# Token places before pair weights, reads of the combined rows on SP and POOL, and weight buffers on the right

## The chip, the core and the metric

The kernel runs on one core of a Trainium2 chip. The metric is the device time of one execution in microseconds (us); less is better. The engines are PE (TensorE, matmuls), DVE (VectorE), ACT (ScalarE), POOL (GpSimd) and SP (SyncE, which here only issues DMAs and takes jumps). Each engine works off its own queue in order, and semaphores join the queues.

## The reference, cut to what matters

Two layers in sequence work on 512 tokens of 1024 values. The first ends in a hierarchical mixture of experts: a group of experts is chosen for each token, then two of its eight experts.

```
def hierarchical_moe(h, w_group, b_group, w_router, b_router, w_gate, w_up, w_down):
    t = h.reshape(-1, d)
    group_prob = softmax(t @ w_group + b_group)
    p_group, g_idx = lax.top_k(group_prob, 1)
    expert_logits = (t @ w_router + b_router).reshape(-1, N_GROUPS, EXPERTS_PER_GROUP)
    ...
    w_top, e_idx = lax.top_k(p_exp, TOP_K)                       # TOP_K = 2
    w_top = w_top / jnp.sum(w_top, axis=-1, keepdims=True) * p_group
    expert_ids = g_idx * EXPERTS_PER_GROUP + e_idx               # 32 experts
    for e in range(N_EXPERTS):
        hid = jax.nn.silu(t @ w_gate[e]) * (t @ w_up[e])         # 1024 -> 256
        out = out + combine[:, e:e + 1] * (hid @ w_down[e])      # 256 -> 1024

x = x + gate2[:, None, :] * ffn                                  # end of the first layer
f = swiglu(rms_norm_2(h, ffn1_norm_pre), ffn1_w_gate, ffn1_w_up, ffn1_w_down)
h = h + 0.5 * rms_norm_2(f, ffn1_norm_post)                      # start of the second
```

The second layer has two such FFNs (2816 wide) around an attention and recurrence mixer.

## The kernel before, in words

x lies in SBUF transposed, as eight tiles of 128 features by 512 tokens. `moe()` computes only the pairs of token and expert that were chosen. It first writes the normalised tokens as rows to DRAM (`h2d`, four DMAs on ACT's queue, line 1082). Routing on DVE gives `rank`, the place of each token in its expert's list (line 1135), and the weights of both experts (`w1`, `w2`, and `wa` spread over the experts).

The 32 experts are taken as eight quads of four. One pass serves the first 32 tokens of each of a quad's four experts, side by side in PE's columns: `expert1(q)` (line 1288) for gate and up, glu (lines 1278 to 1280), `turn` (1297), `expert2(q)` (1325) for down. An expert with more than 32 tokens has a conditional, `more(e)`, whose `wide_pass` serves the further ones; its condition is a count that each engine loads into a register (`count`, line 1380, jump on 1384). In this data a few of the conditionals are taken.

Which tokens stand in a quad is known in two ways. For quads 0 and 1 `select(q)` builds one-hot tiles of the ranks on DVE and multiplies them on PE with `val` (token number, weight, and token number plus 512 for the second choice; line 1227). For the others and for the wide passes a table in DRAM is used, `tab`: `fill_table` writes it with eight indirect scatters on POOL's queue (line 1208), and ACT's queue reads it back into `slots` (lines 1214 and 1202). Either way an indirect DMA on POOL's queue gathers the rows from `h2d` (line 1235) into `xg` for a quad or `htok0` to `htok3` for the wide passes; PE transposes them (1272), ACT and DVE scale them into `xgT` (1260, 1262).

Expert weights come as 192 loads of 512 KB on SP's queue into 30 rotating buffers, 13 in a pool at the left end of SBUF and 17 in one at the right end; a load waits until PE has used its buffer. Results are scattered into `yd` in DRAM, two rows for each token. The last quad's aren't: `combine` adds them by a matmul with one-hot tiles (`sq`, `ys`; lines 1308, 1309, 1313, 1373, 1374). What stands in `yd` is read by `fetch(i)` for 128 tokens at a time, two tiles each (line 1401); `collect(i)` adds both on POOL (1407), transposes on PE (1411) and adds into x on DVE (1415). The first three fetches use six spare weight buffers, the fourth the buffers of the first.

The order in each engine's queue is that of the program, but for what `issue_after` and a scheduler move within it. A conditional with jumps on all engines stands ahead of the last quad (line 1447).

The second layer's weights come as f32 tiles (`wraw`, line 251 on SP's queue), which ACT rounds to `wh` (line 257) and DVE to the rest `wl` (line 258); three matmuls for each product, on `xh`/`wh`, `xl`/`wh`, `xh`/`wl` (lines 274 to 276). `xh` and `xl` are made of x in lines 1590 and 1591. Their pool is `wp2`. The body's end, before:

```
self.xl = [self.t(self.ap, [P, S], f"xl{k}", F32R) for k in range(KT)]
self.wp = pool(s1, "wp2", 4, reuse_waits="tile")
self.even(self.wp, 480)
self.nsplit = 4
self.block2()
```

## Time and profile before

| | us |
|---|---|
| median of 3 runs | 2174.79 |
| lowest and highest run | 2173.87, 2176.84 |
| the profiled execution's own time | 2176.26 |
| its span in the profile | 2174.5 |
| PE busy in it | 1988.9 (91%) |
| DVE, ACT, POOL busy | 1041.9, 703.1, 220.5 |

The span is what the profiler saw of one execution; all starts in the rows count from its beginning. A share of busy time is a mean over stages with different limits, so what bounds a stage is read from that stage.

### The profile page before, as it was taken

What the parts mean: (1) busy time and instruction counts of PE and PEld (TensorE: products, weight loads), DVE (VectorE), ACT (ScalarE), POOL (GpSimd) and SP (SyncE); (2) the same over time, 40 slices, a digit from 0 to 9 for tenths busy, and PEclk for the clock granted to TensorE, in tenths of its full rate; (3) what the DMA queues carried; (4) which work ended last, traced back from release to release, by engine and by line L of the source; (5) the groups of instructions that cost most, each with busy time, mean ns of one, the idle gap of its engine ahead of it and who ended that gap; (6) DMA issues with size and microseconds to landing.
All of it is one profiled execution on the core that took longest, in us unless ns stands there. A gap on an engine that the chain in (4) does not pass through costs nothing. (4 is left out here: it accounts for less than half of the span.)

```text
span 2174.5 us, 32109 instructions
## 1 busy us (share of the span) xinstructions
PE 1988.9 (91%) x12778; PEld 1547.5 (71%) x12778; DVE 1041.9 (48%) x1901; ACT 703.1 (32%) x1173; POOL 220.5 (10%) x243
## 2 busy tenths in 40 slices
PE   5999999777777669999999999999999999999996
PEld 3677777544433348888888788888878888888885
DVE  4763664641111057552355674655664457542443
ACT  3532343122222114322233352524542244322231
POOL 3020002003212121000003200000000041000002
PEclk9999999888999879999999999999999999999998
DMA  7343215366999923333333132323233322333321
GB/s 268 117 127 115 84 58 182 131 229 227 405 394 390 359 83 107 97 89 100 103 97 98 56 100 77 118 63 107 69 102 92 112 69 88 97 93 101 97 87 40
DMA packets 110621, 294.94 MB, mean 136 GB/s; under 512 B 19995, under 2 KB 31387, under 8 KB 110444
## 3 DMA queue, kind: packets, MB, share of 16 engines
q1 hardware_dynamic: 98524, 271.78, 38.2%
q0 software_dynamic: 9856, 14.40, 2.1%
q10 hardware_dynamic: 2064, 6.37, 0.8%
q8 instruction: 113, 1.85, 0.3%
q14 instruction: 64, 0.52, 0.1%
HBM read 296.72 MB, written 17.90 MB: 145 GB/s over the span
## 5 line engine op out<-in xcount | busy, mean ns | idle before, releaser
L274 PE MATMUL mm<-xh,wh 128*128 128x512 f32 (+1 forms) x1584 | 614.6, 390 | 12.1 <-ACT wh L257 8.0
L275 PE MATMUL mm<-xl,wh 128*128 128x512 f32 (+1 forms) x1584 | 604.3, 382 | 4.8 <-DVE xl L1591 4.6
L276 PE MATMUL mm<-xh,wl 128*128 128x512 f32 (+1 forms) x1584 | 601.2, 381 | 0.5 <-DVE wl L258 0.5
L257 ACT ACTIVATE wh<-wraw 128x1024 fp32r<-128x1024 f32 (+3 forms) x282 | 274.0, 974 | 734.8 <-PE mm L275 645.2
L258 DVE TENSOR_TENSOR wl<-wraw,wh 128x1024 fp32r<-128x1024 f32 (+3 forms) x282 | 315.3, 1119 | 185.2 <-ACT wh L257 183.5
L274 PEld LDWEIGHTS mm<-xh,wh 128*128 128x128 f32 x1584 | 301.2, 191 | 78.1 <-ACT wh L257 9.3
L275 PEld LDWEIGHTS mm<-xl,wh 128*128 128x128 f32 x1584 | 302.1, 191 | 60.3 <-DVE xl L1591 6.4
L276 PEld LDWEIGHTS mm<-xh,wl 128*128 128x128 f32 x1584 | 301.2, 190 | 57.8 <-issue 2.0
L340 POOL TENSOR_TENSOR ss<-ss,sq 128x256 f32<-128x256 f32 (+1 forms) x69 | 66.5, 963 | 925.7 <-ACT sq L339 914.4
L274 PE MATMUL mm<-hh,wh 128*128 128x512 f32 (+1 forms) x416 | 148.5, 357 | 0.0
L276 PE MATMUL mm<-hh,wl 128*128 128x512 f32 (+1 forms) x416 | 148.3, 357 | 0.0
L275 PE MATMUL mm<-hl,wh 128*128 128x512 f32 (+1 forms) x416 | 148.2, 356 | 0.0
L1288 PE MATMUL mm<-wmoe,xgT 128*32 128x512 f32 x512 | 72.7, 678 | 26.2 <-DMA wmoe<-in_wmoe 20.3
L275 PEld LDWEIGHTS mm<-hl,wh 128*128 128x128 f32 x416 | 78.6, 189 | 11.4
L274 PEld LDWEIGHTS mm<-hh,wh 128*128 128x128 f32 x416 | 78.6, 189 | 11.3
L276 PEld LDWEIGHTS mm<-hh,wl 128*128 128x128 f32 x416 | 78.6, 189 | 11.2
L1279 DVE SCALAR_TENSOR_TENSOR mth<-mth,mm 128x256 f32<-128x256 f32 x8 | 3.4, 420 | 160.7 <-ACT mth L1278 160.7
L1651 DVE TENSOR_TENSOR sq<-mm,rsb 128x512 f32<-128x512 f32 x44 | 30.4, 691 | 103.9 <-PE mm L276 103.8
L1288 PEld LDWEIGHTS mm<-wmoe,xgT 128*32 128x32 f32 x512 | 20.2, 123 | 76.4 <-issue 40.2
L1646 DVE TENSOR_TENSOR cy<-mm,rsb 128x512 f32<-128x512 f32 x44 | 30.4, 691 | 85.4 <-PE mm L276 83.5
L1837 DVE TENSOR_TENSOR f<-mm,rsb 128x512 f32<-128x512 f32 x24 | 16.4, 688 | 52.1 <-PE mm L276 51.2
L1536 ACT ACTIVATE hh<-cy 128x512 fp32r<-128x512 f32 x44 | 27.9, 633 | 36.8 <-DVE cy L1652 36.8
(509 smaller groups left out, 2602.3 us busy)
## 6 DMA issues: line engine op xcount, KB each, us to landing
wmoe<-in_wmoe SPq DMA_DIRECT2D x192, 512.0 KB
wraw<-in_win SPq DMA_DIRECT2D x90, 512.0 KB
wraw<-in_wgu SPq DMA_DIRECT2D x88, 512.0 KB
wraw<-in_wada SPq DMA_DIRECT2D x32, 512.0 KB
wraw<-in_wd SPq DMA_DIRECT2D x32, 448.0 KB
big<-in_wada SPq DMA_DIRECT2D x16, 512.0 KB
wraw<-in_wd SPq DMA_DIRECT2D x16, 512.0 KB
wraw<-in_wout SPq DMA_DIRECT2D x16, 256.0 KB
```

The costliest lines, as they stand in the source:

```text
L257: self.nc.scalar.activation(h[:, :n], raw[:, :n], AF.Copy)
L258: self.nc.vector.tensor_sub(l[:, :n], raw[:, :n], h[:, :n])
L274: mm(ps, w1, xh[k], start=start and i == 0, stop=False)
L275: mm(ps, w1, xl[k], start=False, stop=False)
L276: mm(ps, w2, xh[k], start=False, stop=stop and i == nk - 1)
L340: self.nc.gpsimd.tensor_add(acc[:, hs], acc[:, hs], sq[:, hs])
L1279: v.scalar_tensor_tensor(th, th, 1.0, gate, op0=ALU.add, op1=ALU.mult)
L1288: self.end1 = mm(ps[cs].rearrange("p a b c -> p (a b c)"), xT[k // 4][:, k % 4, cs], piece(ws[c], k), start=k == 0, stop=k == KT - 1, tile ...
L1536: self.nc.scalar.activation(h, src, AF.Copy, scale=0.5)
L1646: v.tensor_mul(t1, pp[0], rb)
L1651: v.tensor_mul(t2, pp[1], rb)
L1837: v.tensor_mul(dst, ps, rb)
```

## The change: what it does

Routing. `val` loses its weight column, so it no longer needs the weights. `select(0)` stands right behind `rank`, then the gather of quad 0's rows; the weights (`pair_weights`), the table's rows and `fill_table` follow. The weights of quads 0 and 1 are picked by matmuls of their own, `select_weights`, behind `gather(1)`. The one-hot tile of quad 0 lies in a buffer of its own. `count(0)` is issued behind the last scaling of `xgT` on DVE.

Fetch and collect. `fetch` goes from ACT's queue to SP's, the fourth to POOL's. The collects stand between the last quad's conditionals: 0 and 1 behind the second, 2 behind the third, 3 behind the fourth.

Buffers. `wp2` is made at the right end of SBUF, where the 17 weight buffers of the experts lay, and its tiles are laid out before use.

```diff
@@ -1140,51 +1140,56 @@
...
-        val = sm([P, 4, NE, 3], "val")
+        val = sm([P, 4, NE, 2], "val")
...
-        v.tensor_copy(val[:, :, :, 1], wa)
-        v.scalar_tensor_tensor(val[:, :, :, 2], a2, float(S), tokb.unsqueeze(2).to_broadcast([P, 4, NE]), op0=ALU.mult, op1=ALU.add)
...
+        v.scalar_tensor_tensor(val[:, :, :, 1], a2, float(S), tokb.unsqueeze(2).to_broadcast([P, 4, NE]), op0=ALU.mult, op1=ALU.add)
+
+        def pair_weights():
...
+        def table_rows(w1, w2):
...
+            return td, rows
...
-        def fill_table():
+        def fill_table(td, rows):
@@ -1216,20 +1221,31 @@
         def select(q):
 
-            oh = self.t(mp, [P, 4, 4, first], "oh")
+            oh = self.t(mp, [P, 4, 4, first], "oh") if q else q1.rearrange("p (a b c) -> p a b c", a=4, b=4)
             for i in range(4):
                 v.tensor_tensor(oh[:, i], iota[:, :first].unsqueeze(1).to_broadcast([P, 4, first]),
                                 rank[:, i, q::8].unsqueeze(2).to_broadcast([P, 4, first]), ALU.is_equal)
-            pv = self.pst([P, 3], "mm")
+            pv = self.pst([P, 2], "mm")
+            pick(oh, q, pv, val)
+            idu = self.t(mp, [P, 1], "idu", U32, bufs=2)
+            v.tensor_scalar_add(idu, pv[:, 0:1], BIG - 1.0)
+            idx = self.t(mp, [P, 1], "idy", U32, bufs=2)
+            v.tensor_scalar_add(idx, pv[:, 1:2], BIG - 1.0)
+            return idu, idx, oh
+
+        def pick(oh, q, out, vals):
             for i in range(4):
                 for c in range(4):
                     cs = slice(32 * c, 32 * c + 32)
-                    mm(pv[cs, :], oh[:, i, c, :], val[:, i, ex(q, c), :], start=i == 0, stop=i == 3, tile_position=(0, 32 * c))
-            idx = self.t(mp, [P, 1], "idy", U32, bufs=2)
-            v.tensor_scalar_add(idx, pv[:, 2:3], BIG - 1.0)
+                    mm(out[cs, :], oh[:, i, c, :], vals[:, i, ex(q, c)], start=i == 0, stop=i == 3, tile_position=(0, 32 * c))
+
+        def select_weights(q, oh):
+
+            pv = self.pst([P, 1], "mm")
+            pick(oh, q, pv, wa.unsqueeze(3))
             wv = self.t(mp, [P, 1], "wv", bufs=2)
-            v.tensor_copy(wv, pv[:, 1:2])
-            return idx, wv, pv
+            v.tensor_copy(wv, pv)
+            return wv
@@ -1238,9 +1254,7 @@
         def gather(q):
 
             if q < 2:
-                idx, wv, pv = select(q)
-                idu = self.t(mp, [P, 1], "idu", U32, bufs=2)
-                v.tensor_scalar_add(idu, pv[:, 0:1], BIG - 1.0)
+                idu, idx, wv = select(q)
@@ -1259,7 +1273,7 @@
-                    v.tensor_scalar(xTs[hf][:, k, :], pt[:, k, :], self.gs2[:, kk:kk + 1], mod[:, 3, kk:kk + 1], op0=ALU.mult, op1=ALU.add)
+                    self.fed = v.tensor_scalar(xTs[hf][:, k, :], pt[:, k, :], self.gs2[:, kk:kk + 1], mod[:, 3, kk:kk + 1], op0=ALU.mult, op1=ALU.add)
@@ -1398,7 +1412,7 @@
         def fetch(i, ys):
 
             for a in range(2):
-                nc.scalar.dma_start(ys[a], yd[a * S + i * P:a * S + (i + 1) * P, :])
+                (g_ if i == 3 else nc.sync).dma_start(ys[a], yd[a * S + i * P:a * S + (i + 1) * P, :])
             return ys
@@ -1415,10 +1429,14 @@
         gat = {0: gather(0)}
+        w1, w2, wa = pair_weights()
+        fill_table(*table_rows(w1, w2))
         xt = xpose(gat[0][0])
         gat[1] = gather(1)
-        fill_table()
-        count(0)
+        for i in range(2):
+            gat[i] = (*gat[i][:2], select_weights(i, gat[i][2]))
+        with tc.issue_after(self.fed.ins):
+            count(0)
         for c in range(4):
             gather_wide(ex(0, c))
         th = expert1(0, xt)
@@ -1461,10 +1479,10 @@
         for c in range(4):
             more(ex(q, c), late)
-        for i in range(4):
-            collect(i, got[i])
-            if i == 0:
-                got.append(fetch(3, got[0]))
+            for i in ((), (0, 1), (2,), (3,))[c]:
+                collect(i, got[i])
+                if i == 0:
+                    got.append(fetch(3, got[0]))
         expert2(q, hT, *gat[q][1:3], late)
@@ -1958,7 +1976,11 @@
-                self.wp = pool(s1, "wp2", 4, reuse_waits="tile")
+
+                self.even(pool(s1, "gap", reuse_waits="tile"), 480)
+                self.wp = pool(s1, "wp2", 4, side="right", reuse_waits="tile")
+                for n in ("wraw", "wh", "wl"):
+                    self.t(self.wp, [P, 1024], n, F32 if n == "wraw" else F32R, bufs=4)
                 self.even(self.wp, 480)
```

How it moves the instructions. On POOL's queue, at the first quad's gather: `tab` is the table, `xg` the rows of a quad, `htok` those of a wide pass, `h2d` the rows in DRAM. Before:

```order
L1208 DMA tab<-r_td_4881,r_rows_4892 17408x4 x7
L1235 DMA xg_4718<-h2d,idu_4941 128x1024
L1208 DMA tab<-r_td_4881,r_rows_4892 17408x4
L1235 DMA xg_4718<-h2d,idu_4992 128x1024
L1235 DMA htok_751_4735<-h2d,slots_804_4908 128x1024
```

And in the changed kernel:

```order
L1251 DMA xg_4718<-h2d,idu_4891 128x1024
L1213 DMA tab<-r_td_4920,r_rows_4931 17408x4 x8
L1251 DMA xg_4718<-h2d,idu_5013 128x1024
L1251 DMA htok_751_4735<-h2d,slots_793_4863 128x1024
```

The gather for quad 0 stood behind seven of eight scatters, and stands ahead of all of them now.

On ACT's queue, from the conditional ahead of the last quad to its wide pass: `wmoe` are spare weight buffers, `mth` is what glu makes. Before:

```order
L1401 DMA wmoe_8187<-yd 128x1024
L1401 DMA wmoe_8188<-yd 128x1024
L1401 DMA wmoe_8189<-yd 128x1024
L1401 DMA wmoe_8190<-yd 128x1024
L1401 DMA wmoe_8191<-yd 128x1024
L1401 DMA wmoe_8192<-yd 128x1024
L1401 DMA wmoe_8188<-yd 128x1024
L1278 ACTIVATE mth_14994<-mm_14961 128x256
L1299 COPY hT_15001<-mm_14998 128x256
```

And in the changed kernel:

```order
L1465 UNCONDITIONAL_BRANCH
L1292 ACTIVATE mth_15026<-mm_14993 128x256
L1313 COPY hT_15033<-mm_15030 128x256
```

The seven reads ahead of glu left ACT. On SP's queue of the changed kernel they stand behind the same jump, and the next layer's first loads (`wraw`) stand among the jumps of the last quad's conditionals, four more behind them:

```order
L1415 DMA wmoe_8219<-yd 128x1024
L1415 DMA wmoe_8220<-yd 128x1024
L1415 DMA wmoe_8221<-yd 128x1024
L1415 DMA wmoe_8222<-yd 128x1024
L1415 DMA wmoe_8223<-yd 128x1024
L1415 DMA wmoe_8224<-yd 128x1024
L1394 TENSOR_LOAD r_cmi_785_4848
...
L251 DMA wraw_15613<-in_wgu 128x1024
L251 DMA wraw_15619<-in_wgu 128x1024
L1398 COMPARE_AND_BRANCH
L1398 UNCONDITIONAL_BRANCH x2
L251 DMA wraw_15625<-in_wgu 128x1024
```

Before, SP had no read of `yd`, and all loads of `wraw` stood behind the four jumps and a load of `c_cols`. On ACT's queue, at the evictions of the last `expert2` (into `ys`), before:

```order
L1401 DMA wmoe_8187<-yd 128x1024
L1308 ACTIVATE ys_2059_15003<-mm_15453,slots_803_4907 128x512
L1308 ACTIVATE ys_2059_15003<-mm_15464,slots_803_4907 128x512
L339 ACTIVATE sq_15627<-x_68 128x256
```

And in the changed kernel:

```order
L257 ACTIVATE wh_15615<-wraw_15613 128x1024
L1322 ACTIVATE ys_2060_15035<-mm_15485,slots_792_4862 128x512
L257 ACTIVATE wh_15621<-wraw_15619 128x1024
L257 ACTIVATE wh_15627<-wraw_15625 128x1024
L1322 ACTIVATE ys_2060_15035<-mm_15496,slots_792_4862 128x512
L257 ACTIVATE wh_15633<-wraw_15631 128x1024
L339 ACTIVATE sq_15666<-x_68 128x256
```

Four splits of the next layer's weights (`wh`) now stand ahead of, between and behind the two evictions; before, they stood behind x's squares, among the making of `xh`.

## Rows read from the trace of the kernel before

**Rows 1.** Windows: stretch, its length, busy us of each engine, clock, DMA share, GB/s.

```profile
480.00:492.00 12.00, 0.61 (x32) 0.55 (x32) 4.00 (x28) 0.20 (x1) 6.77 (x7) 0.50 0.97 361
...
512.00:536.00 24.00, 21.37 (x123) 13.94 (x127) 2.70 (x8) 5.59 (x13) 4.60 (x5) 0.93 0.85 298
...
560.00:740.00 180.00, 138.22 (x800) 68.25 (x792) 24.72 (x70) 41.16 (x92) 35.40 (x36) 0.93 1.01 391
```

**Rows 2.** Timeline from routing to the first wide pass: start, length, engine, line, operation.

```profile
472.52 0.34 ACTq L1082 DMA_DIRECT2D h2d<-htok  x1
...
479.25 0.29 DVE L1135 SCALAR_TENSOR_TENSOR r_rank<-sm,r_aa 128x128 f32<-128x128 f32 x1 [1.42 <-PE sm L1132]
...
483.40 1.08 POOL L1208 DMA_INDIRECT tab<-r_td,r_rows  x1 [60.71 <-DVE r_td L1186]
...
484.39 0.61 PE L1227 MATMUL mm<-r_val,oh 128*32 128x3 f32 x32 [5.18 <-DVE r_val L1166]
...
491.21 0.97 POOL L1208 DMA_INDIRECT tab<-r_td,r_rows  x1 [0.30 <-issue]
492.05 0.16 DVE L1229 TENSOR_SCALAR idy<-mm 128x1 uint32<-128x1 f32 x1 [7.80 <-remote]
...
493.14 1.06 POOL L1235 DMA_INDIRECT xg<-h2d,idu  x1 [0.95 <-issue]
...
497.38 1.94 PE L1272 MATMUL mm<-c_ident,xg 128*128 128x128 f32 x8 [12.38 <-DMA xg<-h2d,idu]
...
499.69 8.81 PE L1288 MATMUL mm<-wmoe,xgT 128*32 128x512 f32 x64
...
500.00 0.15 DVE L1229 TENSOR_SCALAR idy<-mm 128x1 uint32<-128x1 f32 x1
...
502.82 1.01 POOL L1235 DMA_INDIRECT htok<-h2d,slots  x1 [0.73 <-issue]
...
512.89 1.38 PE L1272 MATMUL mm<-c_ident,htok 128*128 128x128 f32 x8 [1.80 <-ACTq L1384]
```

**Rows 3.** Timeline of the last quad, from its expert1 to the last collect.

```profile
745.27 8.91 PE L1288 MATMUL mm<-wmoe,xgT 128*32 128x512 f32 x64 [5.89 <-ACTq L1447]
...
754.48 10.75 ACTq L1401 DMA_DIRECT2D wmoe<-yd  x7
...
765.27 0.38 ACT L1278 ACTIVATE mth<-mm 128x256 f32<-128x256 f32 x1 [25.02 <-DMA wmoe<-yd]
...
768.53 1.94 PE L1272 MATMUL mm<-c_ident,htok 128*128 128x128 f32 x8 [1.17 <-ACTq L1384]
...
790.87 5.35 PE L1411 MATMUL mm<-c_ident,wmoe 128*128 128x128 f32 x24 [3.39 <-DVEq L1384]
...
796.74 2.34 POOL L1407 TENSOR_TENSOR wmoe<-wmoe,wmoe 128x1024 f32<-128x1024 f32 x1 [26.99 <-DMA wmoe<-yd]
...
799.14 1.10 PE L1411 MATMUL mm<-c_ident,wmoe 128*128 128x128 f32 x8 [2.92 <-POOL wmoe L1407]
```

**Rows 4.** Timeline from the last expert2 to the next layer's first matmul.

```profile
805.61 42.78 SPq L251 DMA_DIRECT2D wraw<-in_wgu  x12
805.62 0.69 ACT L1308 ACTIVATE ys<-mm,slots 128x512 fp32r<-128x512 f32 x1 [0.95 <-PE mm L1325]
...
807.01 6.35 DVE L1374 SCALAR_TENSOR_TENSOR x<-mm,mod,x 128x256 f32<-128x256 f32 x16
...
815.24 1.69 ACT L1590 ACTIVATE xh<-x,c_cols 128x256 fp32r<-128x256 f32 x4
...
816.83 1.04 ACT L257 ACTIVATE wh<-wraw 128x1024 fp32r<-128x1024 f32 x1
...
817.93 0.58 PE L274 MATMUL mm<-xh,wh 128*128 128x256 f32 x1 [5.96 <-ACT wh L257]
```

**Rows 5.** The page's costliest groups: two lines of the next layer's matmuls.

```profile
L274 PE MATMUL mm<-xh,wh 128*128 128x512 f32 (+1 forms) x1584 | 614.6, 390 | 12.1 <-ACT wh L257 8.0
...
L276 PE MATMUL mm<-xh,wl 128*128 128x512 f32 (+1 forms) x1584 | 601.2, 381 | 0.5 <-DVE wl L258 0.5
```

More of the change, by code (lines that the diff above doesn't have):

```diff
@@ L1141, in moe @@
         v.tensor_copy(cmi, cnt)
-        eg = sm([P, 4, 4], "eg")
-        v.tensor_sub(eg, Lg, gm.to_broadcast([P, 4, 4]))
-        s.activation(eg, eg, AF.Exp)
-        pg = sm([P, 4, 1], "pg")
-        v.tensor_reduce(pg, eg, axis=AX.X, op=ALU.add)
-        v.reciprocal(pg, pg)
-        w1, w2 = sm([P, 4, 1], "w1"), sm([P, 4, 1], "w2")
-        v.tensor_sub(w2, m2, m1)
-        s.activation(w2, w2, AF.Exp)
-        v.tensor_scalar_add(w1, w2, 1.0)
-        v.reciprocal(w1, w1)
-        v.scalar_tensor_tensor(w1, w1, 0.5, pg, op0=ALU.mult, op1=ALU.mult)
@@ L1170, in moe @@
-        td = sm([P, 4, 2, 4], "td")
-        tu = td.bitcast(U32)
-        slot = sm([P, 4, NE], "slot")
-        v.scalar_tensor_tensor(slot, rank, float(NE), iota[:, :NE].unsqueeze(1).to_broadcast([P, 4, NE]), op0=ALU.mult, op1=ALU.add)
-        s12, s2 = sm([P, 4, 1], "s12"), sm([P, 4, 1], "s2")
-        a12 = sm([P, 4, NE], "a12")
-        v.tensor_mul(a12, slot, a2)
-        v.tensor_reduce(s2, a12, axis=AX.X, op=ALU.add)
-        v.tensor_mul(a12, slot, aa)
-        v.tensor_reduce(s12, a12, axis=AX.X, op=ALU.add)
@@ L1180, in moe @@
-        v.tensor_sub(s12, s12, s2)
-        rows = self.t(mp, [P, 4, 2], "r_rows", U32)
-        for a, sa in enumerate((s12, s2)):
-            v.tensor_scalar_add(rows[:, :, a:a + 1], sa, -1.0 - NE)
-            v.tensor_scalar_add(tu[:, :, a, 0], tokb, BIG - 1.0)
-            v.tensor_scalar_add(tu[:, :, a, 1], tokb, BIG - 1.0 + a * S)
-            v.tensor_copy(td[:, :, a, 2:3], (w1, w2)[a])
-            v.tensor_scalar_add(td[:, :, a, 3], tokb, BIG)
+        val = sm([P, 4, NE, 2], "val")
@@ new lines, in moe @@
+        v.tensor_copy(val[:, :, :, 0], tokb.unsqueeze(2).to_broadcast([P, 4, NE]))
+        v.scalar_tensor_tensor(val[:, :, :, 1], a2, float(S), tokb.unsqueeze(2).to_broadcast([P, 4, NE]), op0=ALU.mult, op1=ALU.add)
+        def pair_weights():
+            eg = sm([P, 4, 4], "eg")
+            v.tensor_sub(eg, Lg, gm.to_broadcast([P, 4, 4]))
+            s.activation(eg, eg, AF.Exp)
+            pg = sm([P, 4, 1], "pg")
+            v.tensor_reduce(pg, eg, axis=AX.X, op=ALU.add)
+            v.reciprocal(pg, pg)
+            w1, w2 = sm([P, 4, 1], "w1"), sm([P, 4, 1], "w2")
+            v.tensor_sub(w2, m2, m1)
+            s.activation(w2, w2, AF.Exp)
+            v.tensor_scalar_add(w1, w2, 1.0)
+            v.reciprocal(w1, w1)
+            v.scalar_tensor_tensor(w1, w1, 0.5, pg, op0=ALU.mult, op1=ALU.mult)
+            v.tensor_mul(w2, w1, w2)
+            v.tensor_mul(o1, o1, w1.to_broadcast([P, 4, 8]))
+            v.tensor_mul(o2, o2, w2.to_broadcast([P, 4, 8]))
+            v.tensor_add(o1, o1, o2)
+            wa = sm([P, 4, NE], "wa")
+            outer(wa, o1)
+            return w1, w2, wa
@@ new lines, in table_rows @@
+        def table_rows(w1, w2):
+            td = sm([P, 4, 2, 4], "td")
+            tu = td.bitcast(U32)
+            slot = sm([P, 4, NE], "slot")
+            v.scalar_tensor_tensor(slot, rank, float(NE), iota[:, :NE].unsqueeze(1).to_broadcast([P, 4, NE]), op0=ALU.mult, op1=ALU.add)
+            s12, s2 = sm([P, 4, 1], "s12"), sm([P, 4, 1], "s2")
+            a12 = sm([P, 4, NE], "a12")
+            v.tensor_mul(a12, slot, a2)
+            v.tensor_reduce(s2, a12, axis=AX.X, op=ALU.add)
+            v.tensor_mul(a12, slot, aa)
+            v.tensor_reduce(s12, a12, axis=AX.X, op=ALU.add)
+            v.tensor_sub(s12, s12, s2)
+            rows = self.t(mp, [P, 4, 2], "r_rows", U32)
+            for a, sa in enumerate((s12, s2)):
+                v.tensor_scalar_add(rows[:, :, a:a + 1], sa, -1.0 - NE)
+                v.tensor_scalar_add(tu[:, :, a, 0], tokb, BIG - 1.0)
+                v.tensor_scalar_add(tu[:, :, a, 1], tokb, BIG - 1.0 + a * S)
+                v.tensor_copy(td[:, :, a, 2:3], (w1, w2)[a])
+                v.tensor_scalar_add(td[:, :, a, 3], tokb, BIG)
+            return td, rows
```

6 lines of the change are left out of this document (removed).

## The prediction

> **What bounds the kernel now.** I read the windows first. The mixture of experts is the stretch from about 480 to 800 us. From 560 to 740 the DMA share is 1.01 at 391 GB/s, so the weight loads bind there. From 512 to 536 it is 0.85, and the loads follow PE (TensorE), which frees their buffers [rows 1]. The change touches none of these bytes, so that stretch keeps its length and moves with its start. What can be won lies where neither loads nor PE are full: the start, before the first expert matmul, and the tail, after the last weights.
>
> Next the timeline of the start. The rank of each token in its expert is there at 479.25 + 0.29 = 479.54. Then all wait for the token rows of the first quad: PE selects at 484.39, POOL issues seven table scatters from 483.40 to 491.21, VectorE (DVE) reads the selection at 492.05, POOL gathers xg at 493.14, PE transposes xg at 497.38 and begins expert1(0) at 499.69 [rows 2]. POOL's order is what holds: with the places ready at 486, the gather would still stand behind the scatters.
>
> Then the timeline of the tail. PE ends the last quad's expert1 at 745.27 + 8.91 = 754.18. ScalarE (ACT) turns it into glu only at 765.27, after 25.02 us of idleness: ahead of glu on its queue stand seven reads of yd, 10.75 us from the first to the end of the seventh, which waits until POOL has added the first pair. The first wide pass follows at 768.53. Later the collects stop once more: the last pair is added at 796.74, its transposes follow at 799.14 [rows 3].
>
> Last, the handover to the next layer: x ends at 807.01 + 6.35 = 813.36, and PE starts FFN1 at 817.93, released by the weight split wh that ACT ran at 816.83 [rows 4].
>
> **The change part by part.** The sum is made against the profiled execution, 2176.26 us, 1.47 above the median of 2174.79, and moved to the median at the end.
>
> **Routing, the start.** Behind the rank now come four one-hot writes, each of the rank's size (0.29 by its row, 1.2 in all), the selection (0.61) and the reading of the place (0.16) [rows 2]. With 0.3 for three handovers idu is there at 481.8. The gather then waits for h2d, not for its places. The four writes of h2d, 2 MB, begin at 472.52 [rows 2] beside weight loads, in a stretch that moves 361 GB/s [rows 1]; with half of that for h2d they land 11.6 us later, at 484.1, my estimate. So POOL gathers at about 484.3 instead of 493.14.
>
> Its landing is bounded from both sides. From issue to transposes it took 497.38 - 493.14 = 4.2 with the DMA engines almost free, which gives 488.5. On the other side, the loads that fill the engines (share 0.97) belong to the stretch that ends at 492, and 512 KB more add 1.4 at 361 GB/s: 493.4 at the latest. I take 491.5, nearer to the full end. PE's transposes then come 5.9 earlier. Two further selections of one column, 0.61 each at the most, now stand on PE, and the last ACT feed stands behind the slot reads on ACT's queue; I take 0.4 off: **5.5 us**, with 2 and 8 as ends.
>
> Is that carried on? The scatters' pitch is (491.21 - 483.40) / 6 = 1.30. The eighth stood behind xg's gather, at about 494.4; now all eight stand behind it, 484.3 + 8 x 1.30 = 494.7. The wide gathers need the table back and so come 0.3 later, at 503.1 instead of 502.82. Rows gathered then are there 4.2 later, at 507.3. PE wants them 4.4 after the end of expert1(0) (512.89 less 499.69 + 8.81 [rows 2]); with that end near 502.9, at 507.3. It just carries. The count loads on SP come after the last feed now, which delays SP's next weight load only if they are not through when PE frees a buffer, near 505. The arithmetic of the pairs' weights moves behind the places, and nothing needs it before the evictions of expert2(0); cover: all of expert1(0). Without it, 4 us.
>
> **Fetch and collect, the tail.** With yd's reads on SP nothing stands ahead of glu: 754.3 instead of 765.27, **11.0 us**. The wide pass moves to 757.5, the collects from 790.87 to about 779.9. The reads wait for the same scatters and buffers on SP as on ACT, so I leave them at 754.48; the first three additions were done within 10 us of the seventh read and still end before the collects. The four conditionals cost what they did (their jumps show as most of the 3.39 before the collects), but a collect's part now waits for a jump on POOL, PE and DVE each. fetch(3) goes to POOL's queue, its second read behind two jumps. Before, its addition stopped PE for 2.92 [rows 3]; two jumps more lie in its chain now, and two jumps and two collects over it. I take 1 off for all that: **10 us**, with 5 and 11.5 as ends.
>
> A rule of the Trainium skill speaks against POOL as issuer. SBUF — State Buffer, section "SBUF: two separate sides", says that while certain VectorE operations hold the port that they share, GpSimd can't write the descriptors of its DMAs, and gives about 3.1 us instead of 0.62 for one; by it the two reads cost up to 5 more. The trace shows the scatter of 483.40, with DVE at work beside it, at 1.08, and the one of 491.21, with DVE idle, at 0.97 [rows 2]. That is 0.1 apart, and I price it at nothing.
>
> **Weight buffers at the other end, the handover.** The next layer's first weight tiles now lie over buffers that the last quad leaves sooner: in the order SP issues two loads ahead of the fourth conditional and four behind it, so by my estimate near 788 and not after the last expert, as at 805.61 [rows 4]. ACT's first four splits, and two of DVE's, stand around the last expert's evictions. The gain: PE waits for xh, of which the first would be ready near 815.24 + 0.42 = 815.7, and not for wh: 817.93 - 815.7 = 2.2. The cost: two splits of 1.04 stand ahead of the second eviction, which had 0.95 of idleness before it: 1.1, and x ends as much later [rows 4]. Net **1 us**; -3 if wraw lands late behind the reads of yd, 3 if the second eviction hides the splits.
>
> Sum: 5.5 + 10 + 1 = 16.5. That is 2159.8 for the profiled execution, and **2158 us** for the median (2174.79 - 16.5 = 2158.3).
>
> **The rivals.** (1) The start isn't carried. For it: PE's selection ended at 485.0 and DVE read it at 492.05, after 7.80 of idleness for which no engine of the core is named [rows 2]. If that delay belongs to the selection, idu comes near 489, the gather is 4 earlier, not 8.8, and the table, behind it now, is 5 later; 0 to 2 are left, and 2174.79 - 12 = 2163. Against: the second selection was read at 500.00 without such a wait. Chance 0.2. (2) The tail gives part back: the second eviction waits for wraw, or fetch(3) is late by the page's 5, or the jumps between the collects add up to 5. Each costs 4 to 6: 2163. For it speaks that each is a wait on a queue in order, with no other work behind it. Chance 0.15. (3) Both, or a change that doesn't do what it says, because the gather waits for the last loads and the splits for the last expert: 6 or less is left, 2169 to 2177. Chance 0.1. (4) Slower: the new place of the weight tiles makes the next layer's matmuls longer. L274, L275 and L276 have 1584 of the larger kind each, 4752, at 390 and 381 ns [rows 5]. Against a gain of 16.5 it decides from 16500 / 4752 = 3.5 ns each, 0.9%; at 1.5% it is 27 us and 2185. Against: L274 reads wh and L276 wl, tiles at different places, with 2% between them at the most, and L274 is the one that stands first behind each wait. Chance 0.1.
>
> That leaves 0.45 for the forecast.
>
> **How the numbers follow.** By its ends the forecast gains 11 to 22 (not all low ends at once): 2153 to 2164. The range takes in rivals (1) and (2) with their scatter and part of (3): 2151 to 2171 leaves out (4), half of (3) and a small chance of more. Within 0.2% is 4.35 us, about what can be told here from no change. Slower is (4), 0.1; the same is most of (3), 0.07; faster is the rest, 0.83.
>
> **What would show it.** In the changed kernel xg's gather stands ahead of every scatter on POOL, near 484, and expert1(0) begins near 494; if DVE reads the places near 492 all the same, it is rival 1. The first wide pass begins near 507. glu follows the end of the last expert1 within 0.5, and the last collect waits less than 3 for POOL. FFN1's first matmul follows x's end within 3.5, and from it to the end stay 2174.5 - 817.93 = 1356.6 us; if that grew, rival 4. Wrong is the forecast if the way from the rank to the first wide pass shrinks by less than 3, or if glu still waits.

## The result, and the profile after

The changed kernel takes **2160.74 us**, the median of 4 runs (2158.49 to 2163.64). The kernel before took 2175.72 beside it (4 runs), so the ratio is 0.9933, with an interval of 0.9916 to 0.995: faster by 15.0 us. The profiled execution has a span of 2160.6, against 2174.5 before. The forecast was 2158.0.

The start, in the timeline of the changed kernel (columns as in [rows 2]; the weight loads of SP and the last write of `h2d` are shown too):

```profile
478.67 0.29 DVE L1135 SCALAR_TENSOR_TENSOR r_rank<-sm,r_aa 128x128 f32<-128x128 f32 x1 [1.42 <-PE sm L1132]
...
479.41 0.33 ACTq L1082 DMA_DIRECT2D h2d<-htok  x1
...
480.60 0.14 DVE L1231 TENSOR_SCALAR idu<-mm 128x1 uint32<-128x1 f32 x1
...
480.89 33.21 SPq L1045 DMA_DIRECT2D wmoe<-in_wmoe  x10
...
484.73 1.13 POOL L1251 DMA_INDIRECT xg<-h2d,idu  x1 [62.58 <-DMA wmoe<-in_wmoe]
486.16 1.06 POOL L1213 DMA_INDIRECT tab<-r_td,r_rows  x1 [0.30 <-issue]
...
492.86 1.94 PE L1286 MATMUL mm<-c_ident,xg 128*128 128x128 f32 x8 [12.46 <-DMA xg<-h2d,idu]
...
496.83 0.16 PE L1240 MATMUL mm<-r_wa,cy 128*32 128x1 f32 x1 [0.56 <-issue]
...
497.80 0.16 DVE L1231 TENSOR_SCALAR idu<-mm 128x1 uint32<-128x1 f32 x1 [2.23 <-remote]
...
498.40 9.32 PE L1302 MATMUL mm<-wmoe,xgT 128*32 128x512 f32 x62
```

The places (`idu`) are there 1.9 after the rank. The gather of `xg` stands ahead of every scatter and is issued at 484.73, 5.3 after the last write of `h2d`. The row names a weight load as what it waited for. In E9 below, where the six last loads come later, the gather is issued 5.3 after that write too, so these loads are not what held it. Up to here the forecast holds (idu 481.8, gather 484.3). Then the rows land late: transposes at 492.86, 8.1 after the issue. From there to expert1(0) it takes another 5.5, of which more below. From the rank to the first wide pass nothing is won in this execution: 33.67, against 33.64 before.

The tail, in the same timeline (answers to [rows 3]):

```profile
745.01 8.69 PE L1302 MATMUL mm<-wmoe,xgT 128*32 128x512 f32 x64 [6.19 <-ACTq L1465]
...
753.78 0.38 ACT L1292 ACTIVATE mth<-mm 128x256 f32<-128x256 f32 x1 [14.08 <-PE mm L1302]
...
754.24 2.80 SPq L1415 DMA_DIRECT2D wmoe<-yd  x6
...
757.04 1.06 PE L1286 MATMUL mm<-c_ident,htok 128*128 128x128 f32 x8 [1.41 <-DVE sq L1327]
...
763.66 0.60 POOL L1415 DMA_DIRECT2D wmoe<-yd  x1 [0.30 <-POOL wmoe L1421]
...
777.59 0.57 POOL L1415 DMA_DIRECT2D wmoe<-yd  x1 [8.64 <-PE mm L1425]
...
780.85 1.06 PE L1425 MATMUL mm<-c_ident,wmoe 128*128 128x128 f32 x8 [2.69 <-DVEq L1398]
...
784.33 1.97 PE L1425 MATMUL mm<-c_ident,wmoe 128*128 128x128 f32 x8 [2.41 <-POOL wmoe L1421]
```

glu (753.78) follows the end of expert1 (745.01 + 8.69 = 753.70) by 0.08; before it came 11.1 after it. The wide pass begins at 757.04, forecast 757.5. The last collect stops for POOL for 2.41, forecast below 3. Between them is a gain that the forecast did not have. The windows of both kernels over the wide pass (columns: stretch, its length, busy us of PE, PE's weight loads, DVE, ACT and POOL, clock, DMA share, GB/s), before:

```profile
757.00:773.00 16.00, 5.13 (x16) 4.00 (x17) 4.62 (x7) 2.50 (x6) 6.99 (x3) 0.57 0.55 216
```

and after:

```profile
757.00:773.00 16.00, 15.48 (x64) 10.87 (x64) 6.04 (x13) 4.25 (x10) 7.62 (x4) 1.00 0.55 208
```

From the end of expert1 to the wide pass it was 14.4 us before (754.18 to 768.53), in which PE did two transposes only, and the granted clock of the stretch above was 0.57, a mean between the level of 1.2 GHz (0.50) and the full one. It is 3.3 now, with the same two transposes, and the clock stays at 1.00, which is 2.4 GHz. The same ten matmuls at the head of the wide pass, before:

```profile
770.41 3.65 PE L1340 MATMUL mm<-wmoe,cy 128*128 128x256 f32 x10
```

and after:

```profile
758.17 2.43 PE L1354 MATMUL mm<-wmoe,cy 128*128 128x256 f32 x10
```

The clock does not stay up in each kernel with this tail. E4, a run told below, has the same 3.3 us ahead of its wide pass, and yet the mean over the same stretch is 0.89:

```profile
752.00:768.00 16.00, 15.51 (x57) 10.93 (x58) 4.37 (x11) 4.25 (x10) 7.62 (x4) 0.89 0.56 217
```

The ten matmuls take 4.11 there. From its start to the first matmul of `combine` the wide pass takes 14.2 in E4 and E6, 13.6 in E7 and E11, and 12.6 in the seven other profiles in which glu comes early. What decides this is not shown.

The handover, in the timeline after (answers to [rows 4]):

```profile
793.20 0.42 SPq L245 DMA_DIRECT2D c_cols<-in_cols  x1
...
793.76 5.96 DVE L1388 SCALAR_TENSOR_TENSOR x<-mm,mod,x 128x256 f32<-128x256 f32 x15
...
798.92 6.06 POOL L340 TENSOR_TENSOR ss<-ss,sq 128x256 f32<-128x256 f32 x5 [3.11 <-ACT sq L339]
...
799.64 2.35 DVE L258 TENSOR_TENSOR wl<-wraw,wh 128x1024 fp32r<-128x1024 f32 x2
...
802.60 0.42 ACT L339 ACTIVATE sq<-x 128x256 f32<-128x256 f32 x1 [2.50 <-POOL ss L340]
...
804.27 1.22 PE L274 MATMUL mm<-xh,wh 128*128 128x256 f32 x4 [5.95 <-ACT xh L1608]
```

x ends at 799.72 and FFN1 starts 4.55 later, as before (813.36 to 817.93, 4.57). It no longer waits for `wh`, as the change has it, but for `xh`. That stands on ACT behind squares of x (`sq`), and a square waits until POOL has added the ones before to the sum (line 340). Everything behind is as it was: from FFN1 to the end 1356.35 us, against 1356.53, and the two groups of the page that answer to [rows 5]:

```profile
L274 PE MATMUL mm<-xh,wh 128*128 128x512 f32 (+1 forms) x1584 | 614.7, 390 | 12.4 <-ACT xh L1608 10.4
...
L276 PE MATMUL mm<-xh,wl 128*128 128x512 f32 (+1 forms) x1584 | 601.8, 381 | 0.1
```

Cut into sections between the starts of such rows, the spans of five kernels stand like this (us; the next heading says what the other kernels are):

| from, to | before | after | E8 | E2 | E5 |
|---|---|---|---|---|---|
| 0, rank | 479.25 | 478.67 | 477.30 | 479.31 | 479.74 |
| rank, first wide pass | 33.64 | 33.67 | 29.94 | 31.71 | 30.32 |
| to last expert1 | 232.38 | 232.67 | 232.80 | 229.16 | 232.64 |
| to glu | 20.00 | 8.77 | 8.83 | 10.86 | 8.89 |
| to last wide pass | 3.26 | 3.26 | 3.27 | 3.16 | 3.30 |
| to last expert2 | 31.63 | 29.19 | 29.02 | 29.03 | 28.97 |
| to x's end | 13.20 | 13.50 | 13.60 | 12.86 | 12.79 |
| to FFN1 | 4.57 | 4.55 | 4.55 | 4.57 | 4.57 |
| to the end | 1356.53 | 1356.35 | 1356.47 | 1357.17 | 1356.29 |

The third row, where the weight loads bind, lies between 229.2 and 233.1 in the 14 profiles, with kernels of every kind at both ends. It accounts for up to 4 us of what one execution differs from the next. E2's 10.86 to glu is expert1 itself, which takes 10.82 there and 8.69 in the changed kernel.

### The profile page after: what moved, and what is told of

Same layout as the page of the kernel before. It is cut to its first block, busy times and chain, and to the rows that moved or that the text cites. A ratio compares the mean times of both kernels' runs of the same rounds, so it can differ in the third digit from the quotient of the medians.

```text
span 2160.6 us, 32240 instructions
## 1 busy us (share of the span) xinstructions
PE 1988.7 (92%) x12842; PEld 1546.7 (72%) x12842; DVE 1039.1 (48%) x1900; ACT 703.0 (33%) x1173; POOL 223.5 (10%) x245
## 5 line engine op out<-in xcount | busy, mean ns | idle before, releaser
L274 PE MATMUL mm<-xh,wh 128*128 128x512 f32 (+1 forms) x1584 | 614.7, 390 | 12.4 <-ACT xh L1608 10.4
L276 PE MATMUL mm<-xh,wl 128*128 128x512 f32 (+1 forms) x1584 | 601.8, 381 | 0.1
L274 PEld LDWEIGHTS mm<-xh,wh 128*128 128x128 f32 x1584 | 301.4, 191 | 78.5 <-ACT xh L1608 11.4
L276 PEld LDWEIGHTS mm<-xh,wl 128*128 128x128 f32 x1584 | 301.8, 191 | 56.8 <-issue 2.0
L274 PE MATMUL mm<-hh,wh 128*128 128x512 f32 (+1 forms) x416 | 148.5, 357 | 0.0
L276 PE MATMUL mm<-hh,wl 128*128 128x512 f32 (+1 forms) x416 | 148.3, 357 | 0.0
L274 PEld LDWEIGHTS mm<-hh,wh 128*128 128x128 f32 x416 | 78.6, 189 | 11.4
L276 PEld LDWEIGHTS mm<-hh,wl 128*128 128x128 f32 x416 | 78.6, 189 | 11.0
```

Source lines behind the costliest of these rows:

```text
L274: mm(ps, w1, xh[k], start=start and i == 0, stop=False)
L276: mm(ps, w2, xh[k], start=False, stop=stop and i == nk - 1)
```

## The experiments

**Theories.** T1, the forecast's own: the three parts add up, start and tail each from their own wait. T2: the tail carries nearly everything, and the start gives its gain back, to later landing or to a table that comes no sooner. T3: the new place of the weight buffers costs at the handover what it saves.

All kernels compute the whole function. Each group ran on one chip with its own runs of the kernel before.

| | kernel | median | before | ratio (interval) |
|---|---|---|---|---|
| E1 | routing alone | 2171.44 | 2174.53 | 0.999 (0.9981 to 0.9999) |
| E2 | fetch and collect alone | 2160.78 | 2174.53 | 0.9936 (0.9923 to 0.995) |
| E3 | buffers alone | 2182.32 | 2174.53 | 1.0037 (1.0023 to 1.005) |
| E4 | after, pair weights picked later | 2159.47 | 2174.53 | 0.9928 (0.9915 to 0.9942) |
| E5 | after without the buffers | 2158.89 | 2175.44 | 0.992 (0.9907 to 0.9934) |
| E6 | E5, pair weights picked later | 2158.36 | 2175.44 | 0.9919 (0.9906 to 0.9933) |
| E7 | after, four splits on POOL | 2157.61 | 2175.44 | 0.9917 (0.9904 to 0.9931) |
| E8 | after, once more | 2156.07 | 2175.44 | 0.991 (0.9895 to 0.9925) |
| E9 | after, six weight loads held back | 2162.89 | 2174.43 | 0.9948 (0.9935 to 0.9962) |
| E10 | after, collects behind all jumps | 2167.53 | 2174.43 | 0.9969 (0.9957 to 0.9982) |
| E11 | E9, pair weights picked later | 2163.3 | 2174.43 | 0.9949 (0.9935 to 0.9962) |
| E12 | after, a third time | 2159.48 | 2174.43 | 0.9933 (0.9919 to 0.9946) |

The changed kernel itself moved from 2156.07 to 2160.74 between groups. So among E4 to E8 nothing below about 3 us is told apart by the times, and none of them is shown to beat it. What follows about smaller amounts is read from the sections.

### E1 to E3: each part alone

E1 is the kernel before with the routing's hunks of the diff above, E3 that with its last hunk. E2's edit:

```diff
-                nc.scalar.dma_start(ys[a], yd[a * S + i * P:a * S + (i + 1) * P, :])
+                (g_ if i == 3 else nc.sync).dma_start(ys[a], yd[a * S + i * P:a * S + (i + 1) * P, :])
...
             more(ex(q, c), late)
-        for i in range(4):
-            collect(i, got[i])
-            if i == 0:
-                got.append(fetch(3, got[0]))
+            for i in ((), (0, 1), (2,), (3,))[c]:
+                collect(i, got[i])
+                if i == 0:
+                    got.append(fetch(3, got[0]))
```

Expected of E1: 

> Only the routing part, on the kernel before. Theory (the start is not carried: in the changed kernel the first expert matmul came 1.3 us earlier, the first wide pass 0.5, the last quad 0.3): 0.3 to 0.8 us below the kernel before, that is no change that can be measured, and xg gathered near 484.7, the first expert matmul near 498.4, the first wide pass near 512.4. Rival (the start does carry the forecast 5.5 us and the tail alone gives less than it seems): 2170 us.

Expected of E2: 

> Only the reads of yd on SP and POOL and the collects between the conditionals, on the kernel before. Theory (the tail gives all of it: 11.5 us that glu comes earlier, and some 2 to 3 more because the wide pass and the collects then run with the clock high and without the wait for the last addition): 13 to 14.5 us below the kernel before, 2161 to 2163 us, with the wide pass of the last quad near 757 and the way from it to the last collect some 3 us shorter than before. Rival (the tail gives 10 as forecast, the rest comes from the other parts): 2166 us.

Expected of E3: 

> Only the weight buffers at the other end, on the kernel before. Theory (the early splits gain 2 us at the first matmul and lose it again, 1 because two splits stand ahead of the second eviction on ACT, 2 because a DVE split of two SBUF operands stops a POOL addition that the making of xh waits for): within 1 us of the kernel before, with one POOL addition of about 2.8 us instead of 0.72 behind x's last eviction. Rival (the buffers give 1 to 2 us by themselves and another part took it away): 2173 to 2174 us. Other rival (the new places cost the matmuls): over 2180 us.

Measured: -3.1, -13.7 and +7.8 us. Together that would be -9, and the whole change gives -15 to -19. So the parts do not add up, and the one that doesn't fit is the buffers. E2 alone has most of the gain, as T2 has it; E1's 3.1 says that the start keeps a part of its own.

E2 also settles rival 1. Its routing is that of before, and its timeline of the start reads:

```profile
484.44 0.61 PE L1227 MATMUL mm<-r_val,oh 128*32 128x3 f32 x32 [5.17 <-DVE r_val L1166]
...
485.14 0.16 DVE L1229 TENSOR_SCALAR idy<-mm 128x1 uint32<-128x1 f32 x1 [0.84 <-PE mm L1227]
...
492.55 1.06 POOL L1235 DMA_INDIRECT xg<-h2d,idu  x1 [0.30 <-issue]
```

DVE reads the selection 0.7 after PE began it, not 7.7 as in the profile of before [rows 2], and the gather still comes at 492.55, behind the seventh scatter. So the late reading was an accident of one execution and POOL's order did hold, as the prediction said.

In E3 x's end is followed by FFN1 only 6.82 later, and the rest takes 1360.70, 4.2 more than before. Its timeline:

```profile
811.88 8.33 POOL L340 TENSOR_TENSOR ss<-ss,sq 128x256 f32<-128x256 f32 x5 [1.98 <-ACT sq L339]
...
812.60 4.62 DVE L258 TENSOR_TENSOR wl<-wraw,wh 128x1024 fp32r<-128x1024 f32 x4
...
817.84 0.42 ACT L339 ACTIVATE sq<-x 128x256 f32<-128x256 f32 x1 [4.78 <-POOL ss L340]
```

Five additions on POOL take 8.33, and one of them 5.12, in the stretch in which DVE runs four weight splits on end. By the view of line 340 the median addition is 0.73. ACT's squares wait 4.78 for it, then `xh`, then FFN1. This is T3, and more: E3 loses 7.8, where its gain was to be had. The Trainium skill has the rule in SBUF — State Buffer, section "Who interferes with whom": "A DVE instruction with two SBUF inputs contends with a GpSimd instruction that reads SBUF". The split `wl` (from `wraw` and `wh`) is such an instruction, the addition reads SBUF, and the trace agrees. It shows more: the addition does not get its turn between one split and the next, but stands still through all four.

Against the profile of before the sections of E3 give +2.4 up to the last expert2, -1.1 to x's end, +2.3 to FFN1 and +4.2 behind. The first of these is another wait, that of the last collect:

```profile
796.23 2.34 POOL L1407 TENSOR_TENSOR wmoe<-wmoe,wmoe 128x1024 f32<-128x1024 f32 x1 [28.84 <-DMA wmoe<-yd]
...
798.63 1.97 PE L1411 MATMUL mm<-c_ident,wmoe 128*128 128x128 f32 x8 [5.62 <-POOL wmoe L1407]
```

The `wraw` loads come earlier now, at 785.74 and behind, and the last read of `yd` (issued at 790.79) has to share the way with them: from its issue to the addition it takes 5.4 instead of 3.9. PE waits 5.62 for it, where it was 2.92 [rows 3], and from the start of these transposes to expert2 it takes 1.9 instead of 1.0.

### E4, E6: the pair weights behind expert1(0)

The two weight selections on PE are moved behind the first expert's matmuls (`end1` is the last of these):

```diff
-        for i in range(2):
-            gat[i] = (*gat[i][:2], select_weights(i, gat[i][2]))
...
+        with tc.issue_after(self.end1.ins):
+            for i in range(2):
+                gat[i] = (*gat[i][:2], select_weights(i, gat[i][2]))
```

Expected of E4: 

> The changed kernel with the selections of the pairs' weights behind expert1(0) on PE instead of ahead of it; nothing else moves. Theory (the small selections, which PE issues 0.7 us apart while the table's scatters land, hold the first expert matmul): expert1(0) begins near 495.5 instead of 498.4 and the first wide pass 2 to 3 us earlier; 2158 us, 2 to 3 below the changed kernel. Rival (whatever PE issues in that stretch is slow, so the expert matmuls are slow there instead): expert1(0) begins earlier but ends as before near 507.7; 2160.5 us.

Expected of E6: 

> As the run without the buffers, and the selections of the weights behind expert1(0) too. Theory (they hold PE 0.9 us ahead of the first expert matmul, and up to 3 in an execution with a disturbance there): 1 us below the run without the buffers, near 2157 us, the lowest yet. Rival (the first wide pass waits for ACT or the table's rows anyway): the same as the run without the buffers.

From the transposes of `xg` to expert1(0) it takes 2.32 in both, as before the change, against 3.19 in E8 and 3.36 in E12. The selections cost 0.9 to 1.0 there, not 0.4. But from the rank to the first wide pass it takes 29.97 in E4 and 29.84 in E6, against 29.94 in E8. In E4 that says little, for `xg` landed later there and expert1(0) starts 16.5 after the rank as in E8. In E6 it starts at 16.2, and the wide pass wins 0.1. The wide pass waits for its own rows then (`htok`), which come over the table. In E8:

```profile
502.81 0.99 POOL L1251 DMA_INDIRECT htok<-h2d,slots  x1 [0.31 <-issue]
...
507.24 1.28 PE L1286 MATMUL mm<-c_ident,htok 128*128 128x128 f32 x8 [2.38 <-DMA htok<-h2d,slots]
```

PE meets two conditionals before this wide pass, and is through the second by 506.5, so the pass is that of the quad's second expert, and its rows are those of the second of the four gathers. POOL issues that one 1.3 behind the first (501.48), and by the view of this gather alone it lands 4.3 later, at 507.1. That of after left aside, ten profiles have the new routing, and in each of them the wide pass starts 0.1 to 0.2 behind the landing of the second gather.

### E5, E7: the handover

E5 leaves `wp2` where it was. E7 keeps the new place and gives the four splits to POOL:

```diff
-        self.nc.vector.tensor_sub(l[:, :n], raw[:, :n], h[:, :n])
+        (eng or self.nc.vector).tensor_sub(l[:, :n], raw[:, :n], h[:, :n])
...
-        w = [self.weights(ap, 1024) for ap in aps]
+        w = [self.weights(ap, 1024, None if post else nc.gpsimd) for ap in aps]
```

Expected of E5: 

> Routing and fetch/collect as in the changed kernel, the weight buffers as before. Theory (routing gives 2.2 to 3.1 by itself, the tail 13.8, and the buffers cost 1 to 3 beside them): 2158 us, 2 to 3 below the changed kernel, with the first matmul of the next layer 4.6 after x's end as before. Rival (the buffers are worth the forecast 1 us in company of the others, though they cost 7.8 alone): 2161.7 us, 1 above the changed kernel.

Expected of E7: 

> The changed kernel with the rests wl of the next layer's first four weights made by POOL instead of DVE. Theory (a DVE split with two SBUF operands stops the POOL addition of squares, 2.84 instead of 0.72, and ACT's making of xh waits behind it): no POOL addition over 1 us behind x's end, xh 2 earlier, the first matmul near 2.5 after x's end instead of 4.55, 2158.5 us, 2 below the changed kernel. Rival (the splits on POOL, 2.3 each by its additions of the same size, delay the squares as much): 2160.7 us or above.

Both start FFN1 as late after x's end as the changed kernel, 4.57 and 4.54, and each for another reason. In E5 it is the split of the weights, as before:

```profile
800.11 1.04 ACT L257 ACTIVATE wh<-wraw 128x1024 fp32r<-128x1024 f32 x1
801.20 0.58 PE L274 MATMUL mm<-xh,wh 128*128 128x256 f32 x1 [5.97 <-ACT wh L257]
```

In the changed kernel it is the addition on POOL, which the view of line 340 gives over the handover (shortest, median and longest in ns):

```profile
L340 POOL TENSOR_TENSOR ss<-ss,sq x6: 723/729/2844, 795.1 to 804.2; 128x256 f32<-128x256 f32 x6
```

One of six takes 2.84 instead of 0.73, beside two splits of DVE (2.35 together). In E7 no split runs on DVE there, and no addition is longer than 0.97. But E7 makes a wait of its own. Its timeline, and then a row of its waits of SP's queue (who waits for whom, us in all, times, longest):

```profile
789.08 7.05 POOL L258 TENSOR_TENSOR wl<-wraw,wh 128x1024 fp32r<-128x1024 f32 x3 [4.82 <-ACT wh L257]
...
796.54 0.42 SPq L245 DMA_DIRECT2D c_cols<-in_cols  x1
...
800.50 3.30 ACT L1608 ACTIVATE xh<-x,c_cols 128x256 fp32r<-128x256 f32 x8 [0.84 <-DMA c_cols<-in_cols]
```

```profile
SPq L251 <- POOL wl L258: 14.6, 4, 6.8
```

A split takes some 2.4 on POOL and 1.2 on DVE. SP's `wraw` loads need the buffers that the splits read, and `c_cols`, which `xh` needs, stands behind these loads: it is issued at 796.54, just as x ends (796.53), and in the changed kernel 6.5 ahead of x's end. So E7 removes the stop of POOL and shows that it was one, but not what FFN1 would win without it. `xh` stood still for `c_cols` for 0.84, so without that wait alone FFN1 would start near 3.7 after x's end, an estimate. The squares were late as well: POOL starts on their sums at 796.10, just when its third split ends. As to the price of the splits on ACT: from the last expert2 to x's end it takes 13.5 to 13.6 with the new place (after, E8) and 12.8 without it (E5). That is 0.7 to 0.8, where the prediction said 1.1.

### E9, E11: what the gather of xg shares its way with

In the changed kernel SP issues six weight loads (3 MB) between the rank and the gather of `xg`. E9 takes these from SP and issues them on ACT's queue behind the last scaling of quad 0's rows:

```diff
-        load(self.nmw[1])
+        load(self.nmw[1] - 6)
...
+        with tc.issue_after(self.fed_act.ins):
+            load(6, nc.scalar)
```

E11 picks the pair weights later as well.

Expected of E9: 

> The changed kernel with the last six weight loads of the first fill (quad 1's, not needed before 531 us) issued by ACT behind its last feed instead of by SP near 481 to 484. Theory (the gather of xg takes 8 us instead of 4.2 only because these loads share the DMA engines with it, and h2d's writes before it): from the gather's issue to the transposes 4 to 5 us, from the rank to the first wide pass 25 to 27 instead of 30, and 3 to 4 us less in all than the changed kernel beside it. Rival (the stage behind is bound by the loads, so a start that comes earlier is given back there): the first wide pass comes earlier, the last quad does not, and the time is that of the changed kernel.

Expected of E11: 

> Both edits of the start on the changed kernel: six loads held back, and the selections of the weights behind expert1(0). Theory: 0.9 us less than with the loads held back alone from the rank to the first expert matmul; 4 to 5 us below the changed kernel beside it, near 2154. Rival (the loads' stage gives it back): that of the changed kernel.

The views of the DMAs, of E9 first (name, queue, number, KB where known, us from issue to landing; the gather of `xg` in the window from 484 to 486.5, those of `htok` in that from 484 to 516):

```profile
xg<-h2d,idu POOLq DMA_INDIRECT x1, 4.2
...
htok<-h2d,slots POOLq DMA_INDIRECT x4, 9.2
```

and of E8, the changed kernel:

```profile
xg<-h2d,idu POOLq DMA_INDIRECT x1, 7.5
...
htok<-h2d,slots POOLq DMA_INDIRECT x4, 4.3
```

The weight loads are what makes the gather late: without them it lands in 4.2, with them in 7.5. That is shown. But the loads must come at some time, and now they lie over the gathers of `htok`, which need 9.2 instead of 4.3. The timeline of E9:

```profile
492.86 9.09 PE L1302 MATMUL mm<-wmoe,xgT 128*32 128x512 f32 x64
...
500.39 3.15 ACTq L1045 DMA_DIRECT2D wmoe<-in_wmoe  x6
...
502.61 1.02 POOL L1251 DMA_INDIRECT htok<-h2d,slots  x1 [4.58 <-DMA slots<-tab]
...
513.18 1.94 PE L1286 MATMUL mm<-c_ident,htok 128*128 128x128 f32 x8 [7.59 <-DMA htok<-h2d,slots]
```

expert1(0) starts 13.6 after the rank, against 16.6 in E8, and yet the first wide pass starts 34.0 after it, against 29.9. E9 and E11 are some 3.5 us slower than the changed kernel in their group (2162.89 and 2163.3 against 2159.48). From 490 to 498, between the landing of `xg` and the reads of the table, the DMA engines of E9 move 20 GB/s or less; the six loads issued there were not tried.

### E10: the collects behind all conditionals

```diff
-            for i in ((), (0, 1), (2,), (3,))[c]:
-                collect(i, got[i])
-                if i == 0:
-                    got.append(fetch(3, got[0]))
+        for i in range(4):
+            collect(i, got[i])
+            if i == 0:
+                got.append(fetch(3, got[0]))
```

Expected of E10: 

> The changed kernel with all collects behind the four conditionals, as before; the reads stay on SP and POOL. Theory (where the collects stand is worth under 1 us, the reads' queue gives the 13): from the last wide pass to the last expert2 29.5 to 30.5 us instead of 29.1, 0.5 to 1 above the changed kernel beside it. Rival (the jumps between the collects cost the forecast 1 us): 1 us below it. Other rival (the collects between the conditionals are what gives the 2 to 3 us over the forecast of the tail): 3 us above it.

It is 8.0 us slower than E12 in its group. From the last wide pass to the last expert2 it takes 31.85, against 29.0: placing the collects between the jumps is worth 2.8 there. The last read goes into a buffer that the transposes of collect 0 free. From the start of `combine` in the wide pass to the issue of that read it takes 10.1 in E10, 8.0 in E12 and 9.8 before; and from there to the addition 5.0, 4.2 and 3.9. So 2.1 of the 2.8 is the read that is issued later, and the rest its landing beside `wraw` loads, as in E3. A larger part is at the handover. Without the collects between them, the four splits stand together on DVE again, as in E3:

```profile
794.30 8.34 POOL L340 TENSOR_TENSOR ss<-ss,sq 128x256 f32<-128x256 f32 x5 [1.98 <-ACT sq L339]
...
795.03 4.62 DVE L258 TENSOR_TENSOR wl<-wraw,wh 128x1024 fp32r<-128x1024 f32 x4
...
801.93 1.22 PE L274 MATMUL mm<-xh,wh 128*128 128x256 f32 x4 [8.22 <-ACT xh L1608]
...
805.94 1.01 PE L348 MATMUL sm<-c_ones,ss 128*128 128x1 f32 x4 [2.79 <-POOL ss L340]
```

FFN1 starts 6.82 after x's end, to the hundredth what E3 has, and the stretch from there to the end is 1361.98, 5.6 more than in the changed kernel. A part of that can be seen in the last row: the matmul over the sums of squares (line 348) stands on PE ahead of FFN1's further matmuls, and waits for POOL as well; in the changed kernel it runs 14 us after FFN1's start. The clock adds to it: in E10 it is 0.50 in both of the five-us windows from 801.5 on, in the changed kernel 0.50 and 0.92 in those from 804. So E3 and E10 lose at the handover by the same four splits in a row on DVE, and the collects between the jumps are what breaks that row in the changed kernel. They also let the last read start earlier. That is why the buffers cost 7.8 alone and next to nothing in company.

E8 and E12 are the changed kernel again, as controls of their groups.

Expected of E8: 

> The changed kernel once more, beside these runs on the same chip, since they differ by 2 us. Both theories: within 1 us of 2160.7.

Expected of E12: 

> The changed kernel once more beside these runs, as the control for differences of a few us. Both theories: between 2156 and 2161.

## Why the prediction was right

2158.0 was forecast and 2160.74 measured, a gain of 15.0 for 16.5, and the range held it. What was to win at the start and in the tail did win there; the gain of the handover did not come. None of the three terms was of the right size, and their errors went against each other: that the sum came so near is luck in part.

**The start: 5.5 forecast, some 2 to 3 measured, 0 in the profiled execution.** With the new routing, from the rank to the first wide pass it takes 29.8 to 30.6 in the eight profiles that keep the loads on SP and have no disturbance (E1, E4 to E8, E10, E12). With the old routing it is 33.3 (E3) and 31.7 (E2). E1's time gives 3.1, by its interval 0.2 to 4.1. The forecast from the same rows was 507.3 - 479.25 = 28.05, 1.9 less than E8's 29.94. The step that failed is "It just carries", with "Rows gathered then are there 4.2 later, at 507.3". It took the first of the four gathers of `htok`. That one came nearly as forecast (24.2 after the rank in E8, forecast 23.9), but the first wide pass needs the second, which is issued 1.3 later. The rest is 0.3 by which the gathers are late, and 0.2 in landing and start. That end now binds: E9 starts expert1(0) 2.9 earlier than E8, and the wide pass starts no earlier, and in E6 it wins 0.1 of 0.4. The landing of `xg`, 7.2 forecast and 7.7 to 8.3 measured, and the selections, 0.4 forecast and 0.9 to 1.0 measured, were off as well, but do not set the end. The estimate for `h2d`, 484.1, came out well for a reason that it did not have: its fourth write is issued only at 479.41, not with the others.

The profiled execution of the changed kernel has 3.7 less than E8 here, by a disturbance that is told at the end. The prediction called itself wrong if this way shrinks by less than 3. In that execution it did not shrink; in E8 it shrinks by 3.7 and in E12 by 3.2, against the profile of before. Against E3, which has the old routing too, it shrinks by 3.4 and 2.9, and against E2 by 1.8 and 1.2 only: whether this sign is met depends on the execution that is taken for before.

**The tail: 10 forecast, 13.7 measured.** From the start of the last expert1 to that of the last expert2, 54.89 became 41.22. glu gave 11.2 of it, as forecast (11.0). The remaining 2.4 are the step that failed, "I take 1 off for all that", wrong in its sign. From its start to the first matmul of `combine` the last wide pass took 14.53 before and takes 12.56 now, which is 2.0 from the clock that stays up (in E4, E6, E7 and E11 it falls, and 0.3 to 0.9 of this is left). The waits between the jumps are there as forecast (2.69 and 2.41), but collect 0 now comes ahead of the third jump and frees the buffer of the last read, which is issued 1.8 earlier behind the start of `combine`; in E10, without that order, this stretch takes 2.8 more. The forecast had counted the jumps that a collect waits for, and neither the clock nor the buffer that it frees.

**The handover: 1 forecast, between -0.3 and -0.45 measured (after, E8, E12).** The cost was right in kind and too high (0.7 to 0.8 for 1.1). The gain of 2.2 did not come: "PE waits for xh, of which the first would be ready near" 2.3 after x's end. It took ACT's squares on [rows 4] at their old pace, and left out that a split on DVE stops the addition on POOL that a square waits for, and with it ACT. FFN1 within 3.5 of x's end was the one sign of the list that failed outright.

**The rivals.** (1) fell in E2, though its number, 2163, is near what was measured: the start carried half, for the reason told and not for DVE's late reading. (2) did not come: the second eviction does not wait for `wraw`, and the two reads on POOL took 0.60 with DVE idle and 0.57 with DVE adding into x. What the Trainium skill says on DMAs of GpSimd in SBUF — State Buffer, section "SBUF: two separate sides", is not seen with these additions, which read one input from PSUM; beside the splits, which run later, no run here shows it. (3) is refuted by the tail, which won more than forecast. (4) is refuted by the page's rows of L274 and L276 and by 1356.35. That edits fold into each other, so that one part is harmful alone (E3, +7.8) and harmless beside another, stood in no rival.

What stays open: when the clock stays up in the last wide pass; whether the six loads can lie between the gathers; and how much the handover would win if no split ran beside POOL's additions and `c_cols` were still early. The last two were not tried.

## What to carry to other kernels

When an early transfer is brought forward, price it by what is on the DMA engines then, and look for the second chain that ends at the same place: here the wide pass waited for the second gather over the table, and the four experiments on the first chain (E4, E6, E9, E11) won nothing that can be measured. Where several transfers of a kind are issued in a row, find out which of them is waited for. Where idle time on PE is removed, read the granted clock behind it, for the matmuls after it may become shorter too, though not in each kernel here. A part of a change should be measured alone and in company: the order that another part happens to give (collects between splits) can be what keeps it from harm.

## What the runs showed of the hardware

An addition on POOL (128x256, both inputs in SBUF) takes 0.72 to 0.73 alone, 2.84 beside two consecutive DVE subtractions of 128x1024 with two SBUF inputs (2.35 together), and 5.12 to 5.13 beside four (4.62). It waits for the end of the whole row, not of one instruction.

In two of the 14 profiles, that of before and that of after, some instructions came about 0.7 us apart for 5 to 8 us between 488 and 500, where no wait in the rows sets such a pace. In the profile of before they are SP's loads of the counts into registers (line 1380), of which some take 0.70 to 0.71, against 0.26 in the median; DVE reads a selection 7.7 late there. In the profile of after PE's weight selections are issued at 495.17, 496.10, 496.83 and 497.54, with idle time before them that the view puts down to "issue", and DVE reads a selection after 2.23 of waiting (shown above). In E8 all 64 run within 1.1. POOL's scatters kept their pitch of 1.29. In the profile of after it cost some 3.7 us at the first wide pass; the profile of before lost little, since there POOL's scatters were what the gather waited for. What it is was not found.
